# Projections of a two-layer decoder step: other DMA queue for queries' and keys' parts, samples' columns made once, rows fetched sooner

## The chip, the cores and the metric

The kernel runs on one core of one Trainium2 chip. The metric is the device time of one execution in microseconds (us); smaller is better. The kernel before took 3235.59 us, the median of 3 runs (3232.98 to 3238.52).

## The reference, cut to what matters

One inference step of a two-layer trunk: a state-space layer (S5), one shared key and value projection of its result, and a layer of stick-breaking attention with its own queries and gate. It is computed for a prompt of 2048 rows and for 8 samples, which have one new row each and 2048 rows of past keys and values in a paged cache. The part that the change touches:

```python
D_MODEL, SEQ, DEC_BATCH, PAGE_SIZE, N_HEADS, HEAD_DIM = 1024, 2048, 8, 128, 16, 64

def rms_norm(x, g):
    return x * lax.rsqrt(jnp.mean(x * x, axis=-1, keepdims=True) + EPS) * g

def shared_kv(x, c, g_kv, w_mod_kv, b_mod_kv, w_kv):
    shift, scale = ada_mod(c, w_mod_kv, b_mod_kv, 2)
    h = rms_norm(x, g_kv) * (1.0 + scale) + shift
    kv = h @ w_kv                              # (rows, 2048): keys, values
    ...

def sb_mixer(h, keys, vals, q_start, w_in, bias, w_out):
    qz = h @ w_in                              # (rows, 2048): queries, gate
    q, z = ...
    o = sb_attend_blocked(q, keys, vals, bias, q_start)
    return (o * jax.nn.silu(z)) @ w_out

# layer 1, with its own modulation of the same x:
h = rms_norm(x, g_pre_b) * (1.0 + scale_b) + shift_b
y = sb_mixer(h, keys, vals, q_start, w_in_b, sb_bias, w_out_b)
x = x + gate_b * rms_norm(y, g_post_b)
```

Inputs and outputs are float32. Both projections, of queries and gate and of keys and values, take the same normalised rows of x; each sample's row has a scale and a shift of its own.

## The kernel before, in words

The program has four parts: `phase_a1` (S5 layer), `phase_a2` (its output projection), `phase_b1` (queries, gate, keys, values) and `phase_b2` (attention and output). The change lies in `phase_b1`, from about 1091 to 1985 us of the profiled execution. In B1 the program is written once, in one order, and a list scheduler moves instructions of each engine ahead of that order where it thinks them ready; so the position of an instruction on its engine is seen only in the scheduled order.

B1 has 16 steps of 256 rows. Pass 0 (`ps` 0, `t` 0 to 7) makes 8 blocks of queries (`q_block`, weights w0) and 8 blocks of the gate (`z_block`, weights w1) in each step; pass 1 makes 8 blocks of keys (`k_block`) and 2 blocks of values (`v_block`; at `t` 1 a third one for the samples). Every projection is computed as three matmuls of float parts, high by high, high by low and low by high, so a block of queries, gate or keys is 24 matmuls of 256 columns (L78), and a block of values is 48 of 512 columns. At `t` 1 the columns are 264: eight more for the samples.

What comes in: the columns of a step (tiles `hi` and `lo`, feature by row) are made in the step before by `norm_cols`, one eighth at each `next(cols)`. In pass 0 `norm_rows` loads two tiles `x` of rows, squares and scales them (L1039, L1043); TensorE transposes them (L83); ScalarE copies the transposed columns to `xn`, which SyncE stores to `xnT` in DRAM, and makes `h` and `hi` (L1073, L1074). In pass 1 `norm_again` only loads `xn` back (L1050). Tiles `x` and `xn` share two buffers. At `t` 1 `sample_cols` does the same for the 8 samples: load `xs` (L1079), square (L859), scale (L861), 8 transposes into `psC`, then four small operations of VectorE into columns 256 to 263 of `hi` and `lo` (L868 to L871). It runs once in each pass.

What goes out: a block of queries or keys is copied from PSUM to its high part by ScalarE (L1117, or L1145 to `kf` and L1147), the low part is subtracted by VectorE (L1118, L1148), and `parts_out` (L1112) stores both parts in two DMAs per block. Tiles `kq` and `kf` have two buffers each; `v`, `pk` and `xn` out share two. For keys TensorE transposes `kf` one block later (`k_rows`), ScalarE copies the result to `pk` (L1137), and SyncE stores it. Values are copied by ScalarE (L1162) and stored (L1165).

Beside this VectorE goes through the past keys of the samples: `more()` calls for 256 half pages, each a load `kp` of 256 KB, three buffers, a multiplication (L1275) and a sum (L1276). SyncE issues all loads and stores of B1; for each page it first loads the page's number (L1253). PSUM: `psA` has 5 buffers (projections), `psC` 3 (transposes).

The order that the program gives to a fetch of rows is one line of the step's loop:

```python
if f == 0 and nxt:
    xt = self.norm_again(nxt[1]) if nxt[0] and nxt[1] else self.norm_rows(nxt[1])
```

so rows for the next step are fetched behind the first block of a step, and `norm_cols` takes them from block 3 (pass 0) or 2 (pass 1) on.

Of the kernel before, what the change touches and what calls it, by code (L numbers as in the profile page):

```python
# [24 lines left out]
HD = 64  # L25
NPG = 16
KT = 8
# [44 lines left out]
class Kern:  # L72
# [643 lines left out]
    def phase_a1(self):  # L716
# [8 lines left out]
        with ExitStack() as c1:  # L725
# [9 lines left out]
            with ExitStack() as c2:  # L735
                with ExitStack() as ce:
                    early = self.pool(ce, "early")
                    early2 = self.pool(ce, "early2")
                    xp = self.pool(c2, "xp", side="right")
                    sc, sh = self.mod_tiles("a", 2)  # L740
                    with ExitStack() as c3:
                        mp = self.pool(c3, "mwp", side="right")
                        self.silu_c(early)
                        self.vectors(early)
                        b, g = self.vo["b_mod_a"], self.vo["g_pre_a"]
                        for f in range(2):
                            self.mod_finish(self.mod_wide(mp, I["w_mod_a"], f * 512, 512, 4), sh, f * 4, 4, b, None, 0)
                            self.mod_finish(self.mod_wide(mp, I["w_mod_a"], D + f * 512, 512, 4), sc, f * 4, 4, b + 8, g, 1.0)
                            if f == 0:
                                xt = self.x_block(xp, xp, 0)  # L750
                                w = [W(0), W(1)]
                    xq = self.pool(c2, "xq", side="right")
                    self.h_block(xp, 0, xt, sc, sh, range(HS))
                    xt1 = self.x_block(xp, xq, 1)
                    self.h_block(xp, 0, xt, sc, sh, range(HS, KT))
                    self.h_block(xp, 1, xt1, sc, sh, range(HS))
                    xt2 = self.x_block(xp, xp, 2)
                    self.h_block(xp, 1, xt1, sc, sh, range(HS, KT))
                    self.s5_params(early, early2)
                h23 = self.pool(c1, "h23")  # L760
                self.h += [[h23.tile([128, KT, n], FR, name=f"h{cb}{g}") for g in "hl"] for cb, n in ((2, 512), (3, 520))]
                self.h_block(xp, 2, xt2, sc, sh, range(HS))
                xt3 = self.x_block(xp, xq, 3)
                self.h_block(xp, 2, xt2, sc, sh, range(HS, KT))
                self.h_block(xp, 3, xt3, sc, sh, range(KT))
                self.kpad_zero(xp)
                xs = xp.tile([128, D], FT, tag="x", name="xs", bufs=4)[:8]
                nc.sync.dma_start(xs, I["x_sample"].rearrange("a b d -> (a b) d"))
                self.sample_cols(xp, xs, sc, sh, self.h[3][0], self.h[3][1], slice(512, 520))
            with ExitStack() as c2:  # L770
                self.sp = self.pool(c2, "sp", side="right")
                self.linears(wp, ep, w)
# [79 lines left out]
        for _ in mods:  # L852
            pass

    def sample_cols(self, pool, xs, sc, sh, hhi, hlo, cols, extra=None):

        nc = self.nc
        ss = pool.tile([8, 1], FT, tag="sss", name="sss")
# [4 lines left out]
        for k in range(KT):  # L863
            self.tr(p[:, k * 8:(k + 1) * 8], xs[:, k * 128:(k + 1) * 128])
        pv = p[:, :64].rearrange("p (k s) -> p k s", s=8)
        for s_, b_, hi, lo in ([(sc, sh, hhi, hlo)] + ([extra] if extra else [])):
            t = pool.tile([128, KT, 8], FT, tag="sct", name="sct")
            nc.vector.tensor_mul(t, pv, s_[:, :, 1:9])  # L868
            nc.vector.tensor_add(t, t, b_[:, :, 1:9])
            nc.vector.tensor_copy(hi[:, :, cols], t)  # L870
            nc.vector.tensor_sub(lo[:, :, cols], t, hi[:, :, cols].bitcast(FT))  # L871
# [181 lines left out]
    def norm_cols(self, t, xt, mods, keep=None, kept=False):  # L1053
# [6 lines left out]
        def go():  # L1060
            for k in range(KT):
# [12 lines left out]
                nc.scalar.activation(hi[:, k, :256], h, AF.Copy)  # L1074
                (nc.gpsimd if k % 2 or kept else nc.vector).tensor_sub(lo[:, k, :256], h, hi[:, k, :256].bitcast(FT))  # L1075
                yield
            if t == 1:
                xs = xp.tile([128, D], FT, tag="x", name="xs", bufs=2)[:8]
                nc.sync.dma_start(xs, self.x1[SEQ:NC1])  # L1079
                self.sample_cols(xp, xs, sc, sh, hi, lo, slice(256, 264))  # L1080

        n = 264 if t == 1 else 256
        return go(), hi[:, :, :n], lo[:, :, :n]
# [1 line left out]
    def phase_b1(self):  # L1085
# [7 lines left out]
        with ExitStack() as c:  # L1093
            hp1 = self.pool(c, "b1h1", side="right")
            op = self.pool(c, "b1o", 2, side="right")
            sp = self.pool(c, "b1s", side="right")
            self.hp[1] = hp1
            self.sample_setup()
            units = self.sample_keys(sp)
            def fm_block(f, n, h, w):  # L1100
# [4 lines left out]
            def parts_out(o, dst, f, t):  # L1105

                for g in range(2):
                    if dst is self.kT:
                        d = dram(dst, (2 * f + g) * 128 * SEQ + t * 256, [[SEQ, HD], [HD * SEQ, 2], [1, 256]])
                    else:  # L1110
                        d = dram(dst, (f * HD * 4 + g) * SEQ + t * 256, [[4 * SEQ, HD], [2 * SEQ, 2], [1, 256]])
                    nc.sync.dma_start(d, o[g * HD:g * HD + HD].bitcast(FT))  # L1112

            def q_block(f, t, n, h):
                p = fm_block(f, n, h, self.W["w0"])
# [61 lines left out]
            steps = [(ps, t) for ps in range(2) for t in range(8)]  # L1177
            mods = (self.mb, self.mkv)
            h = self.h0
            self.load_w("w1", I["w_in_b"], 2 * D, D)  # L1180
            total = 8 * 2 * NPG + 6
            done = [0, 0]
# [7 lines left out]
            for s, (ps, t) in enumerate(steps):  # L1190
# [3 lines left out]
                for f in range(KT):  # L1194
                    next(cols, None)
                    (k_block if ps else q_block)(f, t, n, h)
                    if s > 1:
                        more()
                    if f == 0 and nxt:
                        xt = self.norm_again(nxt[1]) if nxt[0] and nxt[1] else self.norm_rows(nxt[1])  # L1200
                    if f == (2 if ps else 3) and nxt:
                        cols, *nh = self.norm_cols(nxt[1], xt, mods[nxt[0]], None if nxt[0] else op, nxt[0] and nxt[1])
                if late:
# [10 lines left out]
                if ps == 0:  # L1214
                    for f in range(KT):
                        next(cols, None)
                        z_block(f, t, n, h)
                        if s > 1:
                            more()
# [7 lines left out]
                        v_block(i, t, h)  # L1227
                for _ in cols:
                    pass
                if nxt:  # L1230
                    h = nh
                if (ps, t) == (0, 7):
# [543 lines left out]
```

## Time and profile before

| | us |
|---|---|
| median of 3 runs | 3235.59 (3232.98 to 3238.52) |
| the profiled execution | 3241.37 |
| its span in the trace | 3239.7 |
| TensorE busy / VectorE busy / ScalarE busy / GpSimd busy in the span | 91% / 70% / 40% / 33% |
| mean granted clock of TensorE | 0.965 of full speed |

The profiled execution is one execution of the same program, 5.8 us above the median; 1.7 us of it lie outside of the span. PE is TensorE, DVE VectorE, ACT ScalarE, POOL GpSimd, SP SyncE; SPq and ACTq are the DMA issues of SyncE and ScalarE, which do not count as busy time. A row of idle time names what ended it. The granted clock is a share of full speed: 1.00 is 2.4 GHz, 0.50 is 1.2 GHz.

### The profile page before, as it was taken

Reading aid. Unit: us, or ns where it says so; the run is one execution under the profiler, and the core shown is the slowest. Engines: PE = TensorE matmul, PEld = TensorE weight load, DVE = VectorE, ACT = ScalarE, POOL = GpSimd, SP = SyncE. Lnnn points to the kernel's source line nnn. Section 1 sums busy time; section 2 is a strip of 40 time slices with the busy share of each in tenths; the row PEclk is TensorE's granted clock in tenths of the full one; section 3 lists DMA queues with packets and bytes.
Section 4 is the critical chain, followed back from the end, with each engine's and each line's share of the span. In section 5 each row is a group of like instructions: output and inputs, shape, how many; then the busy total and the mean of one; then the engine's idle time right before and its main releaser. Section 6 shows DMA issues by size and latency. Waiting matters only on the chain.

```text
span 3239.7 us, 57105 instructions
## 1 busy us (share of the span) xinstructions
PE 2961.2 (91%) x19352; PEld 2331.7 (72%) x19352; DVE 2274.9 (70%) x4011; ACT 1308.0 (40%) x2954; POOL 1075.4 (33%) x1481
## 2 busy tenths in 40 slices
PE   7899989999999899898599999898999999999998
PEld 3666667778888799898588887555555566666677
DVE  7799998254434546667666554788888989888864
ACT  3422222232222533233332424565556666555541
POOL 1243433000000100000110103676666767666650
PEclk8999999999999899999799999999999999999999
DMA  7433333565453657667666668776767743333234
GB/s 222 135 96 101 100 99 96 164 180 162 134 140 105 192 149 201 181 192 219 207 184 202 198 192 218 211 211 185 218 203 228 216 147 87 113 108 94 80 106 136
DMA packets 498725, 519.51 MB, mean 160 GB/s; under 512 B 57989, under 2 KB 385958, under 8 KB 498242
## 3 DMA queue, kind: packets, MB, share of 16 engines
q1 hardware_dynamic: 493586, 514.46, 54.1%
q8 instruction: 154, 2.52, 0.3%
q10 hardware_dynamic: 4560, 1.35, 0.2%
q14 instruction: 137, 1.12, 0.1%
q0 software_dynamic: 288, 0.06, 0.0%
HBM read 384.97 MB, written 130.75 MB: 159 GB/s over the span
## 4 chain that ended last, share of the span: by engine, by line
PE 40%; DVE 24%; DMA 14%; issue 6%; POOL 4%; SPq 4%; ACT 4%; DVEq 0%; ACTq 0%; POOLq 0%
PE psA L78 14%; DVE cc L57 6%; PE psB L78 6%; DMA kp<-in_cache_k 5%; PE psA L57 5%; PE psZ L57 5%; PE psO L57 4%; PE psC L57 4%; DVE kp L1275 2%; DVE s L57 2%; DMA vp<-in_cache_v 2%; POOL cc L57 1%; DVE zs L1276 1%; PE psC L78 1%; SPq L1253 1%
## 5 line engine op out<-in xcount | busy, mean ns | idle before, releaser
L57 ACT ACTIVATE s<-psZ,sbias 128x512 f32<-128x512 f32 (+2 forms) x640 | 375.5, 649 | 234.0 <-issue 88.2
L57 POOL TENSOR_SCALAR cc<-s 128x1024 f32<-128x1024 f32 (+3 forms) x320 | 319.9, 1000 | 296.3 <-ACT s L57 289.8
L57 DVE TENSOR_TENSOR_SCAN cc<-cc,zero 128x384 f32<-128x384 f32 (+7 forms) x256 | 338.5, 1343 | 70.6 <-POOL cc L57 70.6
L57 ACT ACTIVATE wT<-psC 128x512 f32<-128x512 f32 (+3 forms) x640 | 311.8, 545 | 180.6 <-PE psC L57 180.5
L57 POOL TENSOR_TENSOR s<-s,cc 128x384 f32<-128x384 f32 (+2 forms) x288 | 332.7, 1155 | 99.1 <-DVE cc L57 82.6
L57 PE MATMUL psZ<-X,Q 128*128 128x512 f32 (+2 forms) x1280 | 357.8, 398 | 0.8 <-ACT s L57 0.5
L57 PE MATMUL psC<-idf,s 128*128 128x128 f32 x2176 | 306.5, 280 | 51.0 <-ACT wT L57 42.0
L57 PEld LDWEIGHTS psC<-idf,s 128*128 128x128 f32 x2176 | 246.0, 143 | 139.4 <-ACT wT L57 53.5
L1075 POOL TENSOR_TENSOR lo<-h,hi 128x256 fp32r<-128x256 f32 x92 | 78.6, 864 | 786.8 <-ACT hi L1074 554.0
L57 DVE TENSOR_TENSOR_SCAN cc<-cc,car,zero 128x1025 f32<-128x1025 f32 x128 | 299.9, 2343 | 50.9 <-POOL cc L57 50.9
L78 PE MATMUL psA<-hi,w0h 128*128 128x256 f32 (+1 forms) x1024 | 304.1, 297 | 12.7 <-ACT w0h L892 4.7
L57 DVE TENSOR_TENSOR s<-s,cc 128x640 f32<-128x640 f32 (+2 forms) x320 | 291.2, 910 | 33.3
L1275 DVE TENSOR_TENSOR kp<-kp,qb 128x512 f32<-128x512 f32 x256 | 181.1, 710 | 187.5 <-DMA kp<-in_cache_k 160.9
L78 PE MATMUL psA<-hi,w0l 128*128 128x256 f32 (+1 forms) x1024 | 294.7, 288 | 1.7 <-DVE w0l L893 1.7
L78 PE MATMUL psA<-lo,w0h 128*128 128x256 f32 (+1 forms) x1024 | 294.8, 288 | 0.2 <-DVE lo L871 0.2
L57 PE MATMUL psO<-wT,V 128*64 128x256 f32 (+1 forms) x2304 | 257.8, 373 | 6.3 <-DVE zb L57 6.3
L57 PEld LDWEIGHTS psZ<-X,Q 128*128 128x128 f32 x1280 | 210.3, 191 | 57.1 <-issue 22.2
L57 PEld LDWEIGHTS psO<-wT,V 128*64 128x64 f32 x2304 | 158.2, 137 | 91.9 <-issue 13.8
L78 PEld LDWEIGHTS psA<-hi,w0h 128*128 128x128 f32 x1024 | 201.1, 196 | 15.6 <-DVE z L1127 5.8
L78 PEld LDWEIGHTS psA<-hi,w0l 128*128 128x128 f32 x1024 | 200.3, 196 | 2.2 <-DVE w0l L893 2.2
L78 PEld LDWEIGHTS psA<-lo,w0h 128*128 128x128 f32 x1024 | 200.9, 196 | 0.8 <-POOL lo L1075 0.5
L1276 DVE TENSOR_REDUCE zs<-kp 128x8 f32<-128x512 f32 x256 | 174.0, 683 | 5.6
(413 smaller groups left out, 6769.2 us busy)
## 6 DMA issues: line engine op xcount, KB each, us to landing
kp<-in_cache_k SPq DMA_DIRECT2D x256, 256.0 KB
vp<-in_cache_v SPq DMA_DIRECT2D x256, 256.0 KB
Q<-qT SPq DMA_DIRECT2D x128, 256.0 KB
x<-x SPq DMA_DIRECT2D x50, 512.0 KB
X<-kT SPq DMA_DIRECT2D x48, 512.0 KB
x<-in_x_prompt SPq DMA_DIRECT2D x32, 512.0 KB
qT<-kq SPq DMA_DIRECT2D x128, 128.0 KB
kT<-kq SPq DMA_DIRECT2D x128, 128.0 KB
```

The lines of the kernel that those rows point to most:

```text
L57: return self.tc.keep_in_program_order(f(*a, **k))
L78: self.nc.tensor.matmul(out, lhsT, rhs, start=start, stop=stop, skip_group_check=True)
L1075: (nc.gpsimd if k % 2 or kept else nc.vector).tensor_sub(lo[:, k, :256], h, hi[:, k, :256].bitcast(FT))
L1253: ld, (r,) = nc.values_load_multi_w_load_instructions(self.pt[:, s * NPG + pg:s * NPG + pg + 1], engines=[mybir.EngineType.SP], min_val=0, ...
L1275: nc.vector.tensor_mul(kp, kp, qb)
L1276: nc.vector.tensor_reduce(zs[:, pg, a * 8:a * 8 + 8], kp.rearrange("p (h d) -> p h d", h=8), axis=mybir.AxisListType.X, op=OP.add)
```

## The change: what it does, and the diff

Three parts, all in B1.

- `parts_out` issues its two stores per block of queries or keys from ScalarE instead of SyncE: 256 DMAs, 128 in each pass.
- `sample_cols` takes several destinations. In pass 0 at `t` 1 it also makes the columns that pass 1 needs (with the modulation `mkv`) into two new small tiles `skv`. In pass 1 at `t` 1 the load of `xs`, the square, the reciprocal root, the 8 transposes and the small operations are gone; two copies of VectorE put `skv` into the columns 256 to 263.
- Rows are fetched half a step sooner: those of step 1 ahead of the loop (ahead of the load of w1), those of step s+2 behind the sixth z block of step s in pass 0 (where `cols` is finished first, so that the tiles `x` are free) or at the end of step s in pass 1.

```diff
@@ sample_cols
-    def sample_cols(self, pool, xs, sc, sh, hhi, hlo, cols, extra=None):
+    def sample_cols(self, pool, xs, *dsts):
...
-        for s_, b_, hi, lo in ([(sc, sh, hhi, hlo)] + ([extra] if extra else [])):
+        for s_, b_, hi, lo, cols in dsts:
@@ norm_cols
-            if t == 1:
+            if t == 1 and kept:
+                for d, p in ((hi, self.skv[0]), (lo, self.skv[1])):
+                    nc.vector.tensor_copy(d[:, :, 256:264], p)
+            elif t == 1:
                 xs = xp.tile([128, D], FT, tag="x", name="xs", bufs=2)[:8]
                 nc.sync.dma_start(xs, self.x1[SEQ:NC1])
-                self.sample_cols(xp, xs, sc, sh, hi, lo, slice(256, 264))
+
+                self.sample_cols(xp, xs, (sc, sh, hi, lo, slice(256, 264)), (*self.mkv, *self.skv, slice(0, 8)))
@@ phase_b1
+            self.skv = [hp1.tile([128, KT, 8], FR, name=f"skv{g}") for g in "hl"]
@@ parts_out
-                    nc.sync.dma_start(d, o[g * HD:g * HD + HD].bitcast(FT))
+                    nc.scalar.dma_start(d, o[g * HD:g * HD + HD].bitcast(FT))
@@ the steps
+            fetch = lambda ps, t: self.norm_again(t) if ps and t else self.norm_rows(t)
+            xt = fetch(*steps[1])
             self.load_w("w1", I["w_in_b"], 2 * D, D)
...
-                    if f == 0 and nxt:
-                        xt = self.norm_again(nxt[1]) if nxt[0] and nxt[1] else self.norm_rows(nxt[1])
...
                     for f in range(KT):
                         next(cols, None)
+                        if f == 6 and s < 14:
+                            for _ in cols:
+                                pass
+                            xt = fetch(*steps[s + 2])
                         z_block(f, t, n, h)
...
                 for _ in cols:
                     pass
+                if ps and s < 14:
+                    xt = fetch(*steps[s + 2])
```

Lines behind the edits move by up to 11, so L1117 of the changed kernel is L1112 of before, L1150 is L1145, L1152 is L1147, L1142 is L1137, L1170 is L1165, L1271 is L1260.

How the scheduled order moves, at the three places that the prediction speaks of. First TensorE at the border from step 0 to step 1 of pass 1, the end of a v block (`w1`) and the start of the first block of keys (`w0`), before:

```order
L78 MATMUL psA<-w1h_18159,hi_17430 128x512 x2
L83 MATMUL psC<-idf,c 1x128 x2
L78 MATMUL psA<-w1l_18160,hi_17430 128x512 x2
L78 MATMUL psA<-w1h_18159,lo_17431 128x512 x2
L83 MATMUL psC<-idf,xs 128x8 x8
L78 MATMUL psA<-hi_18393,w0h_17650 128x264
L78 MATMUL psA<-lo_18394,w0h_17650 128x264
L78 MATMUL psA<-hi_18393,w0l_17651 128x264
```

The same place with the change:

```order
L78 MATMUL psA<-w1h_18170,hi_17437 128x512 x2
L78 MATMUL psA<-w1l_18171,hi_17437 128x512 x2
L78 MATMUL psA<-w1h_18170,lo_17438 128x512 x2
L78 MATMUL psA<-hi_18400,w0h_17657 128x264
L78 MATMUL psA<-lo_18401,w0h_17657 128x264
L78 MATMUL psA<-hi_18400,w0l_17658 128x264
```

The eight transposes of `xs` are gone from between the two blocks, and the keys follow the values directly.

Second ScalarE among the blocks of keys of a later step of pass 1 (`kf`, `kq` and `pk` are a block's results, `h` and `hi` the next step's columns), before:

```order
L1147 ACTIVATE kq<-kf 128x256
L1074 ACTIVATE hi_23147<-h 128x256
L1137 ACTIVATE pk<-psC 128x256
L1073 ACTIVATE h<-xn,mod_kv_6724,mod_kv_6723 128x256
L1074 ACTIVATE hi_23147<-h 128x256
L1145 ACTIVATE kf<-psA 128x256
L1147 ACTIVATE kq<-kf 128x256
L1137 ACTIVATE pk<-psC 128x256
L1145 ACTIVATE kf<-psA 128x256
```

and such a place with the change:

```order
L1152 ACTIVATE kq<-kf 128x256
L1074 ACTIVATE hi_23122<-h 128x256 x2
L1117 DMA kT<-kq 64x2x256 x2
L1150 ACTIVATE kf<-psA 128x256
L1142 ACTIVATE pk<-psC 128x256
L1152 ACTIVATE kq<-kf 128x256
L1073 ACTIVATE h<-xn,mod_kv_6724,mod_kv_6723 128x256
L1117 DMA kT<-kq 64x2x256 x2
L1150 ACTIVATE kf<-psA 128x256
```

The pair of stores stands behind the block's `kq` and ahead of the next block's `kf`; it needs VectorE's subtraction of that block.

Third SyncE in step 1 of pass 1: before, the fetch of `xn` (rows of step 3; the scheduler has put it ahead of its place in the program) stands beside the stores of the values, among page loads (`kp`):

```order
L1253 TENSOR_LOAD pt
L1253 ISA x2
L1050 DMA xn<-xnT 128x4x256
L1165 DMA out_p_v<-v 128x512 x2
L1260 ISA
L1260 DMA kp<-in_cache_k 128x512
```

With the change the fetch of the same rows stands ahead of them, among the stores of the keys' rows (`out_p_k`) of that step:

```order
L1264 TENSOR_LOAD pt
L1264 ISA x2
L1050 DMA xn<-xnT 128x4x256
L1143 DMA out_p_k<-pk 128x2x128
L1050 DMA xn<-xnT 128x4x256
L1143 DMA out_p_k<-pk 128x2x128
```

The two loads have moved from the step's values to its keys. In pass 0 the loads of `x` keep their places on SyncE from the second step on, since the scheduler had moved them ahead before; in the first step they now stand, with three page loads, ahead of the load of w1.

## Rows read from the trace of the kernel before

**Rows 1.** The page, busy time by engine: us, share of the span, instructions.

```profile
PE 2961.2 (91%) x19352; PEld 2331.7 (72%) x19352; DVE 2274.9 (70%) x4011; ACT 1308.0 (40%) x2954; POOL 1075.4 (33%) x1481
```

**Rows 2.** Windows of pass 0 and pass 1; the columns are in the first line.

```profile
core 0: us, PE busy (x) PEld busy (x) DVE busy (x) ACT busy (x) POOL busy (x), PEclk, DMA share, GB/s
1097.00:1500.00 403.00, 371.49 (x3026) 365.80 (x3025) 243.18 (x552) 142.14 (x356) 25.12 (x30) 0.97 0.65 185
1531.00:1967.00 436.00, 382.66 (x2396) 337.02 (x2396) 248.54 (x441) 143.15 (x362) 47.82 (x57) 0.94 0.68 198
```

**Rows 3.** Timeline of PE at pass 1, step 1: start, us, instruction, [idle before <-releaser].

```profile
1607.19 0.99 PE L83 MATMUL psC<-idf,xs 8*128 8x8 f32 x8 [24.31 <-DVE xs L861]
1609.56 0.59 PE L78 MATMUL psA<-hi,w0h 128*128 128x264 f32 x1 [1.38 <-DVE hi L870]
```

**Rows 4.** Timeline of ACT in the same stretch.

```profile
1595.55 0.60 ACT L1162 ACTIVATE v<-psA 128x512 f32<-128x512 f32 x1 [1.94 <-DMA out_p_v<-v]
1600.77 1.06 ACT L859 ACTIVATE jk<-xs 8x1024 bf16<-8x1024 f32 x1 [4.62 <-DMA xs<-x]
```

**Rows 5.** Windows of three stretches at half clock, behind three stalls of PE.

```profile
1607.20:1615.70 8.50, 6.90 (x33) 6.53 (x34) 5.15 (x9) 4.72 (x10) 3.29 (x4) 0.50 0.53 162
1377.70:1383.50 5.80, 5.80 (x28) 5.80 (x29) 5.05 (x9) 2.16 (x6) 0.73 (x1) 0.50 0.72 199
1903.90:1909.20 5.30, 5.30 (x25) 5.30 (x26) 1.71 (x3) 4.13 (x12) 3.36 (x4) 0.50 0.78 221
```

**Rows 6.** Timeline of PE at the first keys of three later steps.

```profile
1735.54 0.69 PE L83 MATMUL psC<-idf,kf 128*128 128x128 f32 x2 [3.17 <-ACT kf L1145]
1843.30 0.44 PE L83 MATMUL psC<-idf,kf 128*128 128x128 f32 x2 [3.51 <-ACT kf L1145]
1903.85 0.69 PE L83 MATMUL psC<-idf,kf 128*128 128x128 f32 x2 [4.32 <-ACT kf L1145]
```

**Rows 7.** Timeline of ACT just before the first and the last of these.

```profile
1729.36 1.09 ACT L1073 ACTIVATE h<-xn,mod_kv,mod_kv 128x256 f32<-128x256 f32 x2 [12.91 <-DMA xn<-xnT]
1899.22 0.42 ACT L1147 ACTIVATE kq<-kf 128x256 fp32r<-128x256 f32 x1 [4.56 <-DMA kT<-kq]
```

**Rows 8.** Waits of ACT: us in total, times, longest.

```profile
ACT kq L1117 <- DMA qT<-kq: 62.3, 22, 10.4
ACT h L1073 <- DMA xn<-xnT: 42.3, 7, 12.9
```

**Rows 9.** Timeline of PE, four stalls of pass 0.

```profile
1123.15 0.90 PE L83 MATMUL psC<-idf,x 128*128 128x128 f32 x3 [4.82 <-DVE x L1043]
...
1322.46 0.69 PE L83 MATMUL psC<-idf,x 128*128 128x128 f32 x2 [4.03 <-ACT h L1073]
...
1377.68 0.69 PE L83 MATMUL psC<-idf,x 128*128 128x128 f32 x2 [3.40 <-ACT h L1073]
...
1480.92 0.44 PE L83 MATMUL psC<-idf,x 128*128 128x128 f32 x1 [5.82 <-DVE x L1043]
```

**Rows 10.** Line L1112: ns of one issue, min/median/max, first and last start.

```profile
L1112 SPq DMA_DIRECT2D kT<-kq x128: 580/597/1237, 1531.0 to 1966.2; - x128
```

**Rows 11.** Timeline of ACT, two blocks of keys without columns between them.

```profile
1622.58 0.39 ACT L1145 ACTIVATE kf<-psA 128x264 f32<-128x264 f32 x1 [2.27 <-PE psA L78]
...
1623.21 0.41 ACT L1147 ACTIVATE kq<-kf 128x256 fp32r<-128x256 f32 x1
...
1625.71 0.39 ACT L1145 ACTIVATE kf<-psA 128x264 f32<-128x264 f32 x1 [2.09 <-PE psA L78]
```

**Rows 12.** Groups of instructions by line: busy us, mean ns of one | idle before.

```profile
L1074 ACT ACTIVATE hi<-h 128x256 fp32r<-128x256 f32 x128 | 51.0, 411 | 6.2 <-PE psA L78 4.4
L1148 DVE TENSOR_TENSOR kq<-kf,kq 128x256 fp32r<-128x256 f32 x64 | 28.4, 444 | 50.9 <-ACT kq L1147 48.1 <-DMA kT<-kq 2.5
L1275 DVE TENSOR_TENSOR kp<-kp,qb 128x512 f32<-128x512 f32 x256 | 181.1, 710 | 187.5 <-DMA kp<-in_cache_k 160.9 <-DMA qb<-qs 25.6
L1276 DVE TENSOR_REDUCE zs<-kp 128x8 f32<-128x512 f32 x256 | 174.0, 683 | 5.6
```

More of the change, by code (lines that the diff above doesn't have):

```diff
@@ L768, in phase_a1 @@
                 nc.sync.dma_start(xs, I["x_sample"].rearrange("a b d -> (a b) d"))
-                self.sample_cols(xp, xs, sc, sh, self.h[3][0], self.h[3][1], slice(512, 520))
+                self.sample_cols(xp, xs, (sc, sh, self.h[3][0], self.h[3][1], slice(512, 520)))
             with ExitStack() as c2:
```

## The prediction

> **What bounds the kernel now.** I read the page first: TensorE is busy for 91% of the span [rows 1], so what can be won is its idle time and its time at a low clock. The windows of the two passes of B1 give the size: 371.49 of 403.00 us and 382.66 of 436.00 us busy, so 31.5 us idle in pass 0 and 53.3 in pass 1, and a granted clock of 0.97 and 0.94 [rows 2]. VectorE, ScalarE and the DMA engines (0.65 and 0.68) are far from full in both, so the idle time is made of waits. TensorE's timeline then says which. The largest is one stall: before step 1 of pass 1 it stands 24.31 us for the samples' rows `xs`, and 1.38 us more for their columns [rows 3]. ScalarE's timeline shows why: the square of `xs` starts at 1600.77, after a wait for the load, which SyncE issues behind pages and stores of values [rows 4]. The clock then stays at 0.50 for 8.5 us [rows 5]. The others are 3 to 6 us each: in pass 1 for `kf`, which ScalarE copies late because it stood in front of `h` for `xn`, or in front of `kq` for a store of `kq` [rows 6, 7]; in pass 0 for `x` or `h` [rows 9]. ScalarE's waits sum these: 62.3 us for stores of queries' parts, 42.3 us for `xn` [rows 8]. Most of that ScalarE absorbs; what reaches TensorE is in rows 6 and 9.
>
> All sums are against the profiled execution, 3241.4 us, which is 5.8 above the median; the forecast is the sum less 5.8.
>
> **Part 1, the samples' columns.** Gone from pass 1: one load, one square, one scaling, 8 transposes. TensorE gets back 24.31 + 1.38 us, and of 8.5 us at half clock one half, 4.2 [rows 3, 5]: 29.9. Some of it comes back as the next wait. The values' last two tiles are copied only when their two buffers have been stored, and the last copy starts at 1595.55 and ends near 1596.2 [rows 4]. The first `kf` is copied behind it. TensorE ran out of work at 1607.19 − 24.31 = 1582.9; with the change it goes on with two blocks of keys, 2 × 3.13 us (1625.71 − 1622.58, [rows 11]), then needs the first `kf` for its transposes, at about 1589. So up to 1596.2 + 0.4 − 1589 = 8 us can be lost there. Nothing is lost if the values' stores, which no longer share SyncE with the keys' parts, come sooner. I take 6, near the upper end, since pages still stand ahead of these stores. **Term: −24, bounds −30 to −22.** What is added, four small operations of VectorE in pass 0 and two copies in pass 1, lies beside TensorE's blocks; their columns are 8 wide, against a subtraction of 256 columns that takes 444 ns [rows 12], so at most 6 × 0.44 = 2.7 us of VectorE, which is free for 160 us of pass 0 (403 − 243, [rows 2]). If it were not free, that 2.7 would be the price. I take 0.
>
> **Part 2, rows fetched sooner.** In pass 1 the two loads of `xn` move from among the values' stores to among the keys', a phase of values ahead. The wait of 12.91 us [rows 7] and its sisters, 42.3 us in 7 waits [rows 8], then go, if the buffers are free. What reached TensorE: 3.17 + 3.51 whole; of the last, 4.32 and half of 5.3 us at half clock (2.65) [rows 5, 6], half, since the wait before it was for a store of `kq`: 3.5. **Term: −10, bounds 0 and −13.7** (3.17 + 3.51 + 4.32 + 2.65). SyncE is passed by two waiting loads: if their buffers are still being read, page loads and stores of values stand behind them; that is the third rival. In pass 0 the order on SyncE hardly moves, so the stalls for `x` (5.82 the largest, [rows 9]) stay. In the first step the rows and three pages (1.05 + 0.79 MB, 9.9 us at 185 GB/s, [rows 2]) go ahead of w1, whose 16 tiles are wanted after 8 blocks: between −4.8 (that step's stall of 4.82, [rows 9]) and 9.9 − 4.8 = +5.1; I take 0, the middle.
>
> **Part 3, stores from ScalarE.** SyncE loses 2 × 0.597 = 1.2 us per block of 3.13 [rows 10, 11], more than a third of its time in a phase of queries or keys, and these stores no longer stand behind page loads that wait for buffers. The stalls that this can take away are those of pass 0 that end on `h`, which ScalarE made late behind `kq`: 4.03 + 3.40, and half of 5.8 us at half clock, 2.9 [rows 5, 9]: 10.3. I take half, since the row names only the last wait of a chain. **Term: −5, bounds 0 and −10.3.** The stalls stand while the DMA engines are busy for 0.65 of the time [rows 2], so there is room to start transfers sooner. Against this speaks the Trainium skill, "DMA: Bandwidth & Descriptors", section "Issuing engines are not separate DMA queues": DMAs started by different engines run on the same 16 engines and interleave, and only the issue time is saved, which is usually small. By that rule this term would be 0 and the forecast 3207.
>
> The price lies on ScalarE. No row shows an issue of such a store there; the nearest is the same store on SyncE, 597 ns [rows 10]. So a block of keys costs ScalarE 1.04 us for `kf`, `pk` and `kq` (1622.58 to 1623.62, [rows 11]), 1.2 us for two issues, and a wait for VectorE's subtraction: at least 0.44, at most a page's product and sum more, 0.71 + 0.68 + 0.44 = 1.84 [rows 12]. I take 0.5, near the lower end, because in pass 1 VectorE is free for 43% of the time (248.54 of 436 busy, [rows 2]) and the scheduled order puts an `h` or `hi` between `kq` and its stores in about half of the blocks, which fills part of the wait. Eight blocks: 8 × 2.74 = 21.9. Some six of the eight columns of the next step lie between them, at 0.55 + 0.41 us [rows 7, 12]: 5.8. Together 27.7, against 8 × 3.13 = 25.0 for TensorE. TensorE can run ahead of ScalarE by about a block less its copies, 3.13 − 1.04 = 2.1, and the phase of values (some 22 us with four copies) lets ScalarE catch up. So 27.7 − 25.0 − 2.1 = 0.6 per step, in 8 steps. **Term: +5, bounds 0 (all hidden) and +90** (0.6 + 8 × 1.34 = 11.3 per step, with 1.84 each time). In pass 0 a block of queries has only one copy, so the stores fit; if the subtraction came late there too, the loss would be of the same size.
>
> **Sum:** 3241.4 − 24 − 10 + 0 − 5 + 5 = 3207.4, less 5.8: about **3202 us** on the scale of the median, 1.0% faster. A difference below 0.2%, 6.5 us, can hardly be told from none here.
>
> **The rivals.**
>
> *Only the samples' stall goes.* Rows that wait for `xn` get the next wait instead, that for `kq` or `pk`, and SyncE's pages are paced by their three buffers anyway. For it: the three stalls of rows 6 name `kf`, with two different waits before it [rows 7]. Against: 12.91 us is far more than what would take its place. 3241.4 − 24 + 5 − 5.8 = 3217.
>
> *All listed stalls go.* 29.9 + 13.7 + 10.3, the two for `x` as well, 4.82 + 5.82 = 10.6, and ScalarE hides its issues: 3241.4 − 64.5 − 5.8 = 3171. For it: there is room on every engine [rows 2]. Against: the `x` loads don't move.
>
> *The samples' stall stays under another name.* SyncE stands at the load of `xn`, now ahead of the values' stores, until ScalarE has read the buffers; the values are stored late, and the copy of `kf` behind them too. Then part 1 gives nothing, part 2 half, and part 3 cancels itself: 3241.4 − 5 − 5.8 = 3231. For it: ScalarE's last copy of values at 1595.55 waits for just such a store [rows 4]. Against: the square of `xs`, 5 us later, is what TensorE waited for.
>
> *ScalarE becomes the pace, and the time is longer.* Its place is the pair of stores behind each `kq`: they wait for VectorE's subtraction, and the next `kf` and the next step's `hi` are queued behind them, for which TensorE waits. The gains of the three parts, 39 us less 5, are eaten when each step loses 34/8 = 4.3 us more, that is at 0.5 + 4.3/8 = 1.0 us of wait per block. At 1.84, a whole page each time, it is 3241.4 − 39 + 90 − 5.8 = 3287. For it: VectorE is busy for 57% of pass 1, and each page is 1.39 us without a break [rows 2, 12], so a subtraction that meets one waits 0.7 on average: 0.57 × 0.7 + 0.44 = 0.84, not far below 1.0. Against: the `h` or `hi` in between, and the pages themselves come late, VectorE stood 160.9 us waiting for them [rows 12], so it often idles just then.
>
> **How the numbers follow.** Forecast 0.44; only the samples' stall 0.22; all stalls 0.13; the stall stays 0.08; ScalarE the pace 0.13. The first three are faster by over 0.2%: 0.79; the fourth lies within 0.2%: 0.08; the last is slower: 0.13. The range goes from 3171, all stalls gone, to 3238, which takes in the rival in which the stall stays and part of ScalarE's bound above the others; left out are most of the last rival and the lower half of the second: about 0.18.
>
> **What would show it.** Right: before step 1 of pass 1 no transposes of `xs`, TensorE idle there by 5 to 8 us and not 24, released by `kf`; the wait of `h` for `xn` near 0; the wait of `kq` for `qT` well below 62 us; ACTq issues of about 0.6 us; pass 1's window some 30 us shorter, pass 0's about 5. Wrong: ScalarE's `kf` or `hi` releasing TensorE in many blocks of a step, with stores waiting for VectorE ahead of them; issues on ScalarE much longer than 0.6 us; or a wait of SyncE at `xn` with values' stores behind it.

## The result, and the profile after

The changed kernel takes 3213.55 us (median of 4 runs, 3209.74 to 3215.04) against 3235.88 us of the kernel before beside it: 0.9929 of it, 95% interval 0.9915 to 0.9944, so 22.3 us less. The forecast was 3202 us, 33.6 less. A second measurement of the changed kernel, with other runs of before beside it, gave 3216.23 against 3233.82 us: 0.9949 (0.9930 to 0.9967), 17.6 us less. The two intervals overlap, so what is to be explained is 18 to 22 us. The profiled execution took 3209.74 us, its span is 3208.0 us.

The page after, busy time by engine, and its DMA queues (packets, MB, share of 16 engines), where q10 now carries the stores that ScalarE issues; before, q1 had 54.1% and q10 0.2%:

```profile
PE 2956.2 (92%) x19344; PEld 2330.9 (73%) x19344; DVE 2265.4 (71%) x4001; ACT 1306.9 (41%) x2952; POOL 1072.4 (33%) x1481
...
q1 hardware_dynamic: 456706, 480.86, 50.2%
q10 hardware_dynamic: 41424, 34.92, 4.0%
```

The same two windows as in [rows 2], after:

```profile
1097.00:1500.00 403.00, 371.15 (x3014) 363.07 (x3012) 261.06 (x570) 138.41 (x348) 23.86 (x30) 0.97 0.67 196
1531.00:1967.00 436.00, 403.20 (x2506) 353.13 (x2507) 221.54 (x404) 142.27 (x367) 47.40 (x61) 0.98 0.68 202
```

Pass 0 is as it was: 371.15 us busy against 371.49. Pass 1 has 403.20 us busy instead of 382.66 at a clock of 0.98 instead of 0.94. So of the two passes only pass 1 gained. TensorE's timeline at the border of its steps 0 and 1, in answer to [rows 3]:

```profile
1584.16 0.63 PE L78 MATMUL psA<-w1h,lo 128*128 128x512 f32 x2
1584.63 0.29 PE L78 MATMUL psA<-hi,w0h 128*128 128x264 f32 x1
```

The 24.31 us are gone, and TensorE goes from values to keys without a stop. ScalarE's waits after, in pass 1 and in pass 0 (us in total, times, longest), in answer to [rows 8]:

```profile
ACT kf L1150 <- issue: 26.3, 14, 6.8
ACT kf L1150 <- DVE kp L1286: 19.0, 9, 3.6
...
ACT kq L1152 <- DMA kT<-kq: 6.4, 7, 1.3
...
ACT h L1073 <- DMA xn<-xnT: 0.8, 2, 0.6
...
ACT kq L1122 <- DMA qT<-kq: 34.4, 14, 4.4
...
ACT kq L1122 <- DVE zs L1287: 22.6, 5, 7.8
```

The waits for `xn` (42.3 us) and for stores of `kq` have nearly gone. In their place stand waits of `kf` and `kq` for VectorE, and "issue", time in which ScalarE waited for nothing that the profile shows. What reaches TensorE, in the same view of its waits from 1500 to 2110 us, that is into the attention's first part, first before, then after:

```profile
PE psC L83 <- DVE xs L861: 24.3, 1, 24.3
PE psC L83 <- ACT kf L1145: 19.3, 9, 4.3
...
PE psC L83 <- ACT pk L1137: 5.3, 1, 5.3
```

```profile
PE psC L83 <- ACT kf L1150: 32.9, 16, 5.6
...
PE psA L57 <- DMA vp<-in_cache_v: 0.3, 1, 0.3
```

So TensorE won 24.3 us, 1.4 us more for the samples' columns, and some 4.2 us of clock behind them (an estimate: half of the 8.5 us at 0.50 in [rows 5]), and it lost 32.9 − 19.3 = 13.6 us to `kf`: 16.3 us net in pass 1. Smaller rows go both ways: a stall of 5.3 us for `pk` in step 0, which the prediction doesn't name, is gone, 3.3 us for the weights `w0h` are new, and the waits for `vp` fell from 2.0 us to 0.3. All rows of this view together, without the clock, fell from 75.6 to 55.8 us, by 19.8, beside 22.3 and 17.6 measured. In a second trace of each kernel (the runs "the change again" and "the kernel before again" below) they are 73.1 and 57.5 us, 15.6 apart.

The largest of the new stalls shows how a store holds ScalarE. ScalarE's timeline in the keys of step 2:

```profile
1656.98 1.25 ACT L1073 ACTIVATE h<-xn,mod_kv,mod_kv 128x256 f32<-128x256 f32 x2
1663.74 1.24 ACTq L1117 DMA_DIRECT2D kT<-kq  x2
1665.02 0.39 ACT L1150 ACTIVATE kf<-psA 128x256 f32<-128x256 f32 x1 [6.80 <-issue]
```

VectorE's timeline at that moment, the last of five pages, then the subtraction that the store needs. VectorE stood 0.44 us for that page's load, so it is the order on VectorE that holds the subtraction, and not only work:

```profile
1661.96 0.69 DVE L1286 TENSOR_TENSOR kp<-kp,qb 128x512 f32<-128x512 f32 x1 [0.44 <-DMA kp<-in_cache_k]
1662.68 0.69 DVE L1287 TENSOR_REDUCE zs<-kp 128x8 f32<-128x512 f32 x1
1663.29 0.42 DVE L1153 TENSOR_TENSOR kq<-kf,kq 128x256 fp32r<-128x256 f32 x1
```

and TensorE's, which had to wait for that `kf`:

```profile
1665.46 0.69 PE L83 MATMUL psC<-idf,kf 128*128 128x128 f32 x2 [5.56 <-ACT kf L1150]
```

ScalarE was done with `h` at 1658.2; the pair of stores starts at 1663.74, when the subtraction is done. Everything behind it on ScalarE waited too. The stall next in size, in step 0, is of another kind:

```profile
1535.41 0.69 PE L83 MATMUL psC<-idf,kf 128*128 128x128 f32 x2 [5.36 <-ACT kf L1150]
```

This is the first `kf` of pass 1. Ahead of it ScalarE makes weights of the values and columns of the next step; the first store of keys starts later, at 1537.3.

A second effect is on the pages. Their products on VectorE (ns of one, min/median/max, first and last start), before and after:

```profile
L1275 DVE TENSOR_TENSOR kp<-kp,qb x256: 665/692/1229, 1179.6 to 1927.0; 128x512 f32<-128x512 f32 x128
```

```profile
L1286 DVE TENSOR_TENSOR kp<-kp,qb x256: 667/691/1235, 1173.7 to 1846.9; 128x512 f32<-128x512 f32 x128
```

The last page comes 80 us sooner (71 against the second trace of before), and the attention starts 24 us sooner.

### The profile page after: what moved, and what is told of

Read it like the earlier page. It is cut to its first block, busy times and chain, and to the rows that moved or that the text cites. A ratio compares the mean times of both kernels' runs of the same rounds, so it can differ in the third digit from the quotient of the medians.

```text
span 3208.0 us, 57055 instructions
## 1 busy us (share of the span) xinstructions
PE 2956.2 (92%) x19344; PEld 2330.9 (73%) x19344; DVE 2265.4 (71%) x4001; ACT 1306.9 (41%) x2952; POOL 1072.4 (33%) x1481
## 3 DMA queue, kind: packets, MB, share of 16 engines
q1 hardware_dynamic: 456706, 480.86, 50.2%
## 4 chain that ended last, share of the span: by engine, by line
PE 37%; DVE 27%; DMA 15%; issue 6%; POOL 4%; ACT 4%; SPq 1%; ACTq 1%; DVEq 0%; POOLq 0%
PE psA L78 14%; DVE cc L57 7%; DMA kp<-in_cache_k 6%; PE psB L78 6%; PE psA L57 5%; PE psZ L57 5%; PE psO L57 3%; PE psC L57 3%; DVE s L57 2%; DVE kp L1286 2%; POOL cc L57 2%; DVE zs L1287 1%; POOL s L57 1%; PE psC L78 1%; DMA vp<-in_cache_v 1%
## 5 line engine op out<-in xcount | busy, mean ns | idle before, releaser
L1287 DVE TENSOR_REDUCE zs<-kp 128x8 f32<-128x512 f32 x256 | 171.9, 681 | 13.5 <-DMA wsD<-ws 9.7
```

What stands on the lines that cost most here:

```text
L1287: nc.vector.tensor_reduce(zs[:, pg, a * 8:a * 8 + 8], kp.rearrange("p (h d) -> p h d", h=8), axis=mybir.AxisListType.X, op=OP.add)
```

## The experiments

All kernels here compute the whole output. They ran in three groups; each group has its own runs of the kernel before beside it, and the ratios go by these. Where a time is a difference from before, it is the difference of the group's medians.

### The stores back on SyncE

The change with one line undone:

```diff
-                    nc.scalar.dma_start(d, o[g * HD:g * HD + HD].bitcast(FT))
+                    nc.sync.dma_start(d, o[g * HD:g * HD + HD].bitcast(FT))
```

> The change without its third part: the stores of queries' and keys' parts go out from SyncE again, samples' columns and the sooner fetch stay. Theory A: the stores on ScalarE cost more than they give, because each pair waits for VectorE's subtraction and holds the next kf (in the changed kernel TensorE lost 11.6 us in the keys of step 0 and 9 us in the keys of step 2 of pass 1, against about 7 won in step 7 and 3 in pass 0); then this kernel is faster than the change by 5 to 12 us: 3202 to 3209. Theory B: the stores on ScalarE are worth what was forecast for them or more, and the two losses come from the sooner fetch, which moves the loads of w_kv and the pages; then this kernel is slower than the change, by 5 to 15 us: 3219 to 3229, and both losses are still there.

3230.87 us, ratio 1.0000 (0.9988 to 1.0013): the first two parts together are worth nothing without the third. Theory A fell. B had the direction, but put too little on the third part: nothing of the gain is left. TensorE waits 27.3 us for `kf` here, and the attention starts badly, which the third experiment shows more plainly.

### Only the stores from ScalarE

The same line the other way, in the kernel before.

> The kernel before with the third part of the change alone. Theory A: slower than before by 0 to 10 us, 3236 to 3246: the stall for the samples' rows of about 24 us stays, one or two steps of pass 1 lose 5 to 10 us each to ScalarE waiting at a store for VectorE. Theory B: faster than before by 5 to 15 us, 3221 to 3231.

3221.78 us, 0.9970 (0.9961 to 0.9979), 8.8 us less: B. Theory A had the samples' stall stay, and B did not say that it would go. It went. TensorE's timeline:

```profile
1583.21 0.74 PE L83 MATMUL psC<-idf,xs 8*128 8x8 f32 x8 [2.90 <-DVE xs L861]
```

ScalarE's, where the square of `xs` now starts ahead of the values' copies, and SyncE's, where the load is issued among the pages of the keys, before and in this kernel:

```profile
1569.68 1.04 ACT L859 ACTIVATE jk<-xs 8x1024 bf16<-8x1024 f32 x1
```

```profile
1598.68 0.33 SPq L1079 DMA_DIRECT2D xs<-x  x1
```

```profile
1555.34 0.38 SPq L1079 DMA_DIRECT2D xs<-x  x1
```

In the kernel before the square started at 1600.77 [rows 4]. Without any change to the samples' work, 24.31 us have become 2.90. What SyncE is rid of in pass 1 is the issue of 128 stores, at 597 ns some 76 us, and its waits for VectorE at them, 39.5 us in these rows of before:

```profile
SPq L1112 <- DVE kq L1148: 15.6, 15, 4.7
SPq L1112 <- DVE zs L1276: 12.0, 12, 3.8
SPq L1112 <- DVE kp L1275: 11.9, 11, 2.6
```

The list scheduler also placed the load sooner. In the trace of before, all eight stores of the step's key rows and two of its values stand ahead of it on SyncE; here four of the former do, and none of the latter. Which of the three (issues, waits, place in the order) removes the stall was not tried apart. The waits of TensorE from 1500 us on, and of ScalarE in pass 1, in this kernel:

```profile
PE psC L83 <- ACT kf L1145: 31.9, 17, 5.5
```

```profile
ACT h L1073 <- DMA xn<-xnT: 2.5, 2, 1.8
```

So the waits for `xn` go with the stores as well, though this kernel's program fetches rows where the kernel before does. In these two rows of TensorE 24.3 − 2.9 = 21.4 us are won and 31.9 − 19.3 = 12.6 lost, 8.8 net. That this is the measured difference is chance: all rows of the view fall by 17.0 us, from 75.6 to 58.6.

### Only the samples' columns

`sample_cols` and the `t == 1` branch of `norm_cols` from the diff, the rest as before.

> The kernel before with the first part alone, the samples' columns for both passes made in the first. Theory A (the whole gain of the change is this part): faster than before by 24 to 35 us, 3201 to 3212, with no wait of TensorE over 8 us at the border of steps 0 and 1 of pass 1. Rival, that the stall only changes its name as long as the stores of keys' parts share SyncE's queue with the values' stores and xn: 3220 to 3236, with TensorE idle there by over 10 us.

3223.15 us, 0.9971 (0.9959 to 0.9983), 7.4 us less: the time that the rival gave, but without its stall, so neither expectation. In the trace the stall is gone and none stands in its place at the border. From its first matmul (1083.56) to the attention's first instruction on ScalarE (1961.0) B1 takes 877.4 us, against 907.3 and 899.7 in the two traces of before and 887.3 and 889.4 in the two of the change. So in B1 this part alone wins 22 to 30 us, as was forecast for it. But from there to the end of the span it takes 1257.6 us, against 1252.0 and 1245.3 before, and 1244.1 and 1245.1 with the change. The loads of the samples' past values, `vp`, show it (issues on SyncE, first and last start), in this kernel, in the one with stores back on SyncE, in before (second trace) and in the change:

```profile
L1265 SPq DMA_DIRECT2D vp<-in_cache_v x256: 332/333/1182, 1962.8 to 2602.2; - x128
```

```profile
L1271 SPq DMA_DIRECT2D vp<-in_cache_v x256: 332/333/1155, 1973.4 to 2610.8; - x128
```

```profile
L1260 SPq DMA_DIRECT2D vp<-in_cache_v x256: 332/333/1024, 1932.7 to 2606.2; - x128
```

```profile
L1271 SPq DMA_DIRECT2D vp<-in_cache_v x256: 332/333/948, 1918.3 to 2589.0; - x128
```

In the two kernels with part 1 and all stores on SyncE, the first `vp` is issued 2 us after the attention has begun; in the others some 45 us ahead of that. TensorE then waits, in the first of them:

```profile
PE psA L57 <- DMA vp<-in_cache_v: 6.7, 5, 3.2
```

In the scheduled order of these two kernels the loads of `vp` stand behind B1's last stores of values, in the others ahead of the last ones. That the order alone makes the difference was not tried by itself.

### Only the sooner rows

The `fetch` lines of the diff, the rest as before.

> The kernel before with the second part alone, rows fetched sooner. As forecast: 10 us faster, 3226, the three stalls of rows 6 gone. Theory A leaves it 0 to 10 us faster, 3226 to 3236. Theory B, that this part brought the losses: slower than before by 5 to 20 us, 3241 to 3256.

3228.75 us, 0.9995 (0.9985 to 1.0006): nothing. The samples' stall is there with 24.9 us, and ScalarE's waits for `xn` have not even become shorter:

```profile
ACT h L1073 <- DMA xn<-xnT: 47.8, 9, 11.9
```

### Everything but the sooner rows

The change with the `fetch` lines undone.

> The change without its second part: samples' columns and stores from ScalarE, rows fetched where they were before. Theory C (after the first four runs: what bounds these steps is SyncE's queue, the stores on ScalarE empty it, and with it empty the place of the fetch hardly matters): within 5 us of the changed kernel. Rival: the sooner fetch is worth its 10 us as soon as the queue is free, so this kernel is 6 to 12 us slower than the change.

3219.15 us, 0.9949 (0.9932 to 0.9967), exactly the ratio of the changed kernel in this group. Theory C held. ScalarE's wait for `xn` here:

```profile
ACT h L1073 <- DMA xn<-xnT: 1.8, 2, 1.2
```

With the stores off SyncE, rows come in time from either place (waits of 0.8 and 1.8 us). With all stores on it they are late from either: 42.3 and 47.8 us without the samples' columns, 15.7 and 21.6 us with them.

### The keys' low parts on GpSimd

```diff
-                nc.vector.tensor_sub(o[:, 1], kf[:, :256], o[:, 0].bitcast(FT))
+                nc.gpsimd.tensor_sub(o[:, 1], kf[:, :256], o[:, 0].bitcast(FT))
```

(in `k_block` alone)

> The change, with the subtraction for the low part of the keys on GpSimd instead of VectorE (the queries' stay). Theory D (ScalarE, standing at a pair of stores for a subtraction that is queued behind pages on VectorE, holds kf): TensorE's waits for kf in pass 1 fall from 32.9 us to under 15, the stalls of 5.6 and 2.6 us in the keys of step 2 go, and the time is 10 to 18 us below the change. Rival: it is ScalarE's own time, two issues of 0.6 us per block, that makes kf late: waits for kf stay over 25 us, time within 4 us of the change.

3223.95 us, 0.9970 (0.9957 to 0.9982), some 8 us slower than the change in the same group. Theory D fell, and the rival was too mild. Waits of TensorE, and of ScalarE in pass 1:

```profile
PE psC L83 <- ACT kf L1150: 37.1, 20, 4.4
```

```profile
ACT kf L1150 <- issue: 41.2, 19, 2.7
ACT kf L1150 <- POOL lo L1075: 18.8, 12, 2.1
```

The long wait for VectorE is gone (longest 4.4 instead of 5.6), but many short ones took its place, among them 18.8 us behind GpSimd's own `lo` of the next columns.

### The stores one block later

Each pair is kept back and put, by a dependency that only the scheduler sees, behind the next block's copy from PSUM:

```diff
+            held = []
+            def flush(behind=None):
+                while held:
+                    parts_out(*held.pop(), behind)
...
-                parts_out(o, self.kT, f, t)
+                held.append((o, self.kT, f, t))
```

with `flush` called behind the copy to `kf` (or `kq` of a query) and at the end of a step's blocks.

> The change, with each pair of stores of queries' and keys' parts put behind the next block's copy from PSUM on ScalarE, so that VectorE has a block's time (3.1 us) for the subtraction, which stays on VectorE. Theory D: as with the subtraction on GpSimd, waits for kf in pass 1 under 18 us, and waits of ScalarE for VectorE in pass 0 well below the 55 us of the change (kq behind VectorE: 22.6 + 11.1 + 7.3 + 6.5, and more), 8 to 20 us below the change. Rival: with two buffers of kq the copy now waits for the stores to land, the wait only changes its name, and the time is within 4 us of the change.

3212.88 us, 0.9925 (0.9901 to 0.9949), beside 0.9949 (0.9930 to 0.9967) of the change in its group: not told apart from it. `kf` no longer waits for VectorE, yet TensorE's waits for it are as long, and ScalarE's have changed their name:

```profile
PE psC L83 <- ACT kf L1161: 32.5, 18, 4.9
```

```profile
ACT kq L1163 <- DMA kT<-kq: 47.3, 20, 4.3
ACT kq L1163 <- DVE kp L1298: 16.5, 7, 3.8
```

The two buffers of `kq` are now what ScalarE waits for, as the rival said.

### The change again

> The changed kernel itself, beside the three above on the same chip: 0.99 to 0.995 of the kernel before, with the losses in the keys of steps 0 and 2 of pass 1 in its trace again, if they belong to the program and not to one execution.

3216.23 us, 0.9949 (0.9930 to 0.9967). TensorE's waits for `kf` are 35.5 us, the longest 6.15 in step 0 and 6.01 in step 2: the two losses belong to the program, and that of step 0 again has no store of keys ahead of it.

### Only the queries' stores from ScalarE

```diff
-                    nc.scalar.dma_start(d, o[g * HD:g * HD + HD].bitcast(FT))
+                    (nc.sync if dst is self.kT else nc.scalar).dma_start(d, o[g * HD:g * HD + HD].bitcast(FT))
```

> The change, with only the queries' parts stored from ScalarE; the keys' parts go out from SyncE as before. Theory E (the gain of the stores' move is that SyncE gets through its page loads sooner, and it is made in pass 0: in the changed kernel the 128th page is multiplied at 1495 and the last at 1847, before at 1574 and 1927): the pages keep that lead to within 20 us, TensorE's waits for kf in pass 1 fall below 28 us since ScalarE issues nothing there, and the time is between the change and 8 us less. Rival F (SyncE is short in pass 1 itself, where values, xn and pages share it): most of the gain is lost, 10 to 20 us slower than the change, and the loads of vp for the attention come late again (waits of TensorE for vp of 5 us and more at its start).

3210.44 us, 0.9940 (0.9924 to 0.9956): as fast as the change. TensorE's waits, two of its stalls, ScalarE's waits in pass 1, and the pages' products:

```profile
PE psC L83 <- ACT kf L1150: 19.4, 10, 6.1
```

```profile
1807.57 0.69 PE L83 MATMUL psC<-idf,kf 128*128 128x128 f32 x2 [2.71 <-ACT kf L1150]
...
1861.21 0.44 PE L83 MATMUL psC<-idf,kf 128*128 128x128 f32 x2 [4.28 <-ACT kf L1150]
```

```profile
ACT h L1073 <- DMA xn<-xnT: 43.8, 7, 12.5
```

```profile
L1286 DVE TENSOR_TENSOR kp<-kp,qb x256: 665/692/1254, 1174.7 to 1893.4; 128x512 f32<-128x512 f32 x128
```

Waits for `kf` fall by 13.5 us, as theory E said: this is the price of the keys' stores on ScalarE, net of what comes back. For waits for `xn` are back with 43.8 us. Most of that costs nothing, but the two stalls shown, 7.0 us together, stand right behind waits of ScalarE for `xn` (12.45 and 6.98 us). The longest stall, 6.13 us, is the first `kf` of step 0 again, so it is no price of the keys' stores. Half of the pages' lead is lost in pass 1 (last one at 1893.4, between 1846.9 and 1927.0), where E had allowed 20 us.

### Only the keys' stores from ScalarE

The same with the two queues exchanged.

> The change, with only the keys' parts stored from ScalarE; the queries' parts go out from SyncE as before. Theory E: the lead of the pages is lost (128th at about 1570), and with it most of the gain: 8 to 18 us slower than the change. Rival F: within 5 us of the change.

3210.60 us, 0.9938 (0.9924 to 0.9952): the same again, as F said and E did not. TensorE's waits for `kf` are the longest of this group, 38.3 us in 21 stalls, and the last page comes at 1852.0. So either half of the stores, moved, is worth what both are. The intervals leave room for some 7 us between these two versions (estimated from their half-widths, 0.0016 and 0.0014).

### The keys' stores from GpSimd's queue

As the one before last, with `nc.gpsimd` for the keys in place of `nc.sync`.

> The change, with the keys' parts stored from GpSimd's queue, the queries' from ScalarE. If ScalarE's two issues per block of keys and its wait for VectorE are what makes kf late (32.9 us of TensorE's waits in pass 1), they go from ScalarE without coming back to SyncE: waits for kf under 20 us, 6 to 15 us below the change. Rival: GpSimd makes the low parts of the next step's columns, and a store that waits there for VectorE holds them and, through h, ScalarE: waits for h and lo appear, within 4 us of the change or slower.

3214.36 us, 0.9951 (0.9936 to 0.9966): the rival. Waits of TensorE, and of ScalarE in pass 1:

```profile
PE psC L83 <- ACT kf L1150: 23.0, 7, 6.2
```

```profile
ACT kq L1152 <- DMA kT<-kq: 51.5, 27, 5.0
...
ACT h L1073 <- POOL lo L1075: 18.0, 26, 3.2
```

### The kernel before again

> The kernel before once more, for a second trace: its stall for the samples' rows is again between 20 and 28 us, and the 128th and the last page come at about 1574 and 1927, if these belong to the program and not to one execution.

The stall for `xs` is 24.3 us again, TensorE's waits for `kf` are 18.3 us, and the 128th and the last page come at 1567.7 and 1918.2, 7 and 9 us sooner. This execution took 3225.21 us, 16 us less than the profiled one that the forecast was worked out from: up to the attention it is 9.5 us shorter (B1 itself 7.6), and from there on 6.7 us. So a single trace against another says nothing of differences below some 10 us; the stall of 24 us is no matter of chance, the sum of small ones may be.

## Why the prediction was right, and where its steps were not

The time lies in the range, faster, and two thirds of the forecast gain came (22.3 of 33.6 us; 17.6 in the second measurement). The largest term was the right one: the stall for the samples' rows is what the change wins. The other terms were not what came, and that the sum is no further off is partly luck. In the trace part 1 gave 30 us instead of 24, parts 2 and 3 gave nothing of the 10 and the 5 where these were looked for, and the price of the stores was near 14 instead of 5: −30 + 14 = −16 stands for −24 − 10 − 5 + 5 = −34. The range, 67 us wide, would have held many other sums.

**Part 1, −24.** Right in its stage. The stall went, and the give-back of 6 us did not come: TensorE does not stop at all at the border, neither in the change nor with the samples' columns alone, where two copies of values near the border still wait 1.4 and 0.9 us for a store. So the term was nearer to its bound of −30, and with this part alone B1 is 22 to 30 us shorter. The step looked no further than B1: alone the part wins 7.4 us of the whole, outside of its bounds, since the attention after it takes 6 to 12 us longer. And the step put the stall down to the samples' work, while it nearly goes without a change of that work: the stores from ScalarE alone bring it down to 2.90 us. So two parts remove the same stall, each has a loss of its own (a late `vp`, a late `kf`), and together the stall is won once and the loss at `vp` is gone. The gains of the three parts alone, 7.4, 1.8 and 8.8 us, happen to add up to 18.0, beside 17.6 and 22.3 of the change. They are not independent for that: parts 1 and 2 together are worth nothing (1.0000).

**Part 2, −10.** Wrong in its mechanism. The waits for `xn` did go from 42.3 to 0.8 us in the changed kernel, but the stores take them away (2.5 us in the kernel with the stores alone), and the sooner fetch alone leaves them at 47.8. And the sooner fetch was worth nothing in time, alone (0.9995) or beside the other two parts (0.9949 with it and without). What failed is the step from an earlier fetch to rows that come in time. The price of the waits was nearer: with 43.8 us of them, in the kernel with only the queries' stores on ScalarE, two stalls of 7.0 us in all stand behind them, where the step had 3.17 + 3.51 + 3.5. Whether TensorE would be busy sooner without them was not tried. The bound of 0 was the right end.

**Part 3, the gain of −5 in pass 0.** TensorE is busy for the same time in pass 0 as before. ScalarE's wait for `qT` fell from 62.3 to 34.4 us, and the waits of the same copies for VectorE rose: 22.6 us for page sums alone, 5.1 before. Of the stalls in [rows 9] the one of 3.40 went, that of 4.82 gave way to one of 2.70 for w1, and two are there again with 4.38 and 5.69 us. The gain of part 3 alone lies in pass 1 and is the samples' stall. Beside part 1, which removes that stall too, most of it lies behind B1: with the stores back on SyncE the trace is 4.5 us longer in B1 (891.8 against 887.3) and 13.4 us longer from the attention on (1257.5 against 1244.1). No term has this. The rule of the Trainium skill that was set against this step ("DMA: Bandwidth & Descriptors", section "Issuing engines are not separate DMA queues") is borne out in its first half: the transfers took 54.1% of the engines' time before on one queue, and 50.2 + 4.0% on two. Its second half, that only the issue time is saved and that this is usually small, does not fit: part 3 alone is 0.9970, and SyncE was rid of some 76 us of issues in pass 1, which is not small, and of 39.5 us of waits for VectorE at these stores; loads of `xs` and `xn` no longer stood behind them, and pages came 80 us sooner at the end. How much of the gain is the issue time and how much the waits was not separated.

**Part 3, the price of +5.** Mis-sized: 13.6 us more of TensorE's waits for `kf` in the changed kernel (35.5 against 18.3 us in the second traces, 17.2 more), and 13.5 us fewer when the keys' stores go back to SyncE, though 7.0 us behind `xn` come back there. An issue costs on ScalarE what it did on SyncE, as assumed:

```profile
L1117 ACTq DMA_DIRECT2D kT<-kq x128: 582/608/1587, 1537.3 to 1944.2; - x128
```

Too small was the wait for VectorE, taken as 0.5 us for each block alike. It differs much from block to block: in step 2 five pages stood ahead of the subtraction, and the next `kf` came 6.8 us late, which held TensorE for 5.56 us. That is the mechanism of the rival in which ScalarE sets the pace, not in each step: five of the eight lost 5 to 9 us to `kf`, the others under 1. But the subtraction is not the whole of it: the stall of 5.36 us in step 0 has no store ahead of it, and with the subtraction on GpSimd, or with a block's time to spare, `kf` was as late. What ScalarE has to do per block, issues among it, is left as the cause; it was not taken apart further.

**What would show it.** No transposes of `xs`, `xn` waits near 0, issues of 0.6 us: seen. Also the wait of `kq` for `qT` well below 62 us: 34.4. Pass 0 shorter by 5 us, `kf` holding TensorE for 5 to 8 us at the border: not seen; the sign named for the opposite case, `kf` releasing TensorE in many blocks with stores ahead that wait for VectorE, was there: 16 stalls, that of step 0 without such a store.

**Left open:** why part 2, worth nothing by itself, costs part 1 its gain as long as the stores are on SyncE (0.9971 alone, 1.0000 together). The loss lies in B1, which takes 891.8 us instead of 877.4, while the rest is the same (1257.5 and 1257.6 us, with a late `vp` in both); the traces show more waits for `kf` there (27.3 us against 12.5). Which of the moved loads does it was not tried, nor what the late `vp` costs by itself. No version that was run is faster than the change beyond its interval.

## What to carry to other kernels

A long wait for one small load may be a symptom of the queue that it stands in: before rewriting what is loaded, look at what waits ahead of it there, and whether another edit of the same change empties that queue, since a stall that two edits remove is won once. Follow the gain to the end of the program: an edit can win 22 to 30 us in its stage and lose part of it in the next, where a load now comes late. A wait that stands last on an engine off the critical path is worth only what the next one behind it leaves, so price its removal from zero upwards. A store moved to a compute engine's queue brings its own wait along: ask what that store waits for, look for the longest such wait and not only the mean, and see who is queued behind.

## What was not expected of the hardware

Stores issued by ScalarE take as long per issue as by SyncE (median 608 ns and 597 ns), with single ones up to 1.6 us, and the pair in the trace above kept the next copy back for the whole of its wait. The kernel before differed by 16 us between two profiled executions of the same program, 9.5 us of it up to the attention, with the same large stall in both.
